# The neighbourhood values of two hybrid layers projected beside the first differential head

## The chip, the core and the metric

The kernel runs on one core of a Trainium2 chip. The core has a matrix engine (PE, with a weight loader PEld), a vector engine (DVE), a scalar engine (ACT), a general engine (POOL), and a queue of transfers that the kernel issues on SP. Each engine works through its own list of instructions in order and waits where an instruction needs what another engine has not finished. The metric is the time of one execution in microseconds; a change is judged by the median of several executions.

## The reference, cut to what matters

Two layers of a hybrid mixer (sequence 1024, width 1024) are followed by a second network that the change does not touch. A layer projects its normalized input once, splits the result, runs three attentions and projects their gated outputs back:

```python
proj = h @ w_in
c_q, c_kv, k_pe, na_qkv, diff_qkv, g_mla, g_na, g_diff = jnp.split(proj, IN_SPLITS, axis=-1)
...
qn, kn, vn = jnp.split(na_qkv, 3, axis=-1)          # 6 heads of 64
o_na = neighborhood_attention(qn, kn, vn, na_rpb, NA_DIM ** -0.5)
...
qd, kd, vd = jnp.split(diff_qkv, 3, axis=-1)        # 4 heads, 2 x 32 for q and k, 64 for v
# per block of 128 queries:
s = jnp.einsum('bqhnd,bkhnd->bhnqk', qi, k) * scale
p = jax.nn.softmax(s, axis=-1)
a = p[:, :, 0] - lam * p[:, :, 1]
o = jnp.einsum('bhqk,bkhe->bqhe', a, v)
```

`vn`, the neighbourhood values, is `h` times 384 columns of `w_in`. The differential attention needs only `qd`, `kd` and `vd`; the neighbourhood attention, which comes after it in the kernel, is the first to need `vn`.

## The kernel before

Everything is a chain of stages. A stage has items (one step of the outer loop each) and a preparation (loads and splits of weights, loads of queries and keys) that runs spread over the items of the stage ahead of it. An item is a generator: at each step of the chain the new item runs to its first `yield`, and then every unfinished older item runs on to its next `yield` (`lane`, `step`). So a `yield` inside an item means "one item later". A stage may carry a side lane: another list of stages whose items are stepped in even proportion between the items of the main lane; what is left of it is run out when the main stages it is tied to end (`run`).

The order that this writes down is not quite the order in which the engines work. The build sorts each engine's instructions by a simulated timeline (`schedule_with_timeline_sim=True`): an instruction that is written later but ready earlier may go first, and the written order is a priority. Each engine then keeps to that list on the chip.

In a hybrid layer `project1` returns eight projection stages: lat, gate1, gate0, dv, dqk, nq, nk, nv. The last, nv, has 8 items, one for each 128 rows. An item multiplies its rows by the 384 columns: eight blocks of the sum, each as three products of high and low parts, 24 matmuls of 128x384. Its result lies in one half of a PSUM tile named S (`acc` hands out the two halves of one tile to two items in turn); one item later `v_store` copies it out with two ACT casts and two DVE subtractions and stores it. All projections read the layer's input `hT`, 16 SBUF pages; the split weights of nv take 8 pages more. The pool `pg` has 43 pages in all.

After the projections come 4 differential heads, 6 neighbourhood heads and 6 latent heads. A differential head has 16 items: 8 blocks of 128 queries, two items for each, one for either softmax. An item issues two score matmuls into an S tile (there are two S tiles), then DVE takes the row minimum into a page P, one item later ACT takes the exponential and POOL rescales. With the second item of a block POOL adds the two pages (for blocks 0, 3 and 6 of a head DVE does it, one item later). Then the block, called a tile below, waits `lag` items, PE transposes it in 8 matmuls and ACT copies the transposes out; `lag2` items later, for each second block, PE multiplies the pair by the values (16 matmuls in the trace, which shows each as two). The lines of the profile that belong to this are L289 (projection), L297 and L298 (casts and subtractions of the store), L1073 (scores), L793 (row minimum), L796 (exponential), L801 and L1080 (rescaling and addition on POOL), L1083 (addition on DVE), L816 and L822 (transposes and their copies) and L842 (values).

The preparation of the stage nv holds its 4 weight loads and splits, and in layer 0 a quarter of the modulation steps, in layer 1 a quarter of the steps that build tables for the second network. The preparation of head 0 holds constants (6 small loads that keep their order), queries, keys, values and gates, and in layer 1 five further table steps (`step_m`, `step_w`, `step_e`, `step_lv`, `step_k`).

Of the kernel before, what the change touches and what calls it, by code (L numbers as in the profile page):

```python
# [56 lines left out]
def bcast(ap, n=128):  # L57

    return bass.AP(tensor=ap.tensor, offset=ap.offset, ap=[[0, n]] + list(ap.ap))
# [101 lines left out]
class Net:  # L161
# [878 lines left out]
    def diff_stages(self, i, D, mixT):  # L1040
        nc, I = self.nc, self.I
        lam_init = 0.8 - 0.6 * math.exp(-0.3 * i)
        C = {}

        def consts():
            lv = self.small([128, 4, 32], name="lamv")
            for j, nm in enumerate(("lam_q1", "lam_k1", "lam_q2", "lam_k2")):
                self.dma(lv[:, j, :], bcast(I[nm][i]), True)
            lp = self.small([128, 2, 32], name="lamp")
            ls = self.small([128, 2], name="lams")  # L1050
            nlam = C["nlam"] = self.small([128, 1], name="nlam")
            nc.vector.tensor_mul(lp[:, 0, :], lv[:, 0, :], lv[:, 1, :])
            nc.vector.tensor_mul(lp[:, 1, :], lv[:, 2, :], lv[:, 3, :])
            nc.vector.reduce_sum(ls, lp, axis=AX.X)
            nc.scalar.activation(ls, ls, AF.Exp)
            nc.vector.tensor_sub(nlam, ls[:, 1:2], ls[:, 0:1])
            nc.vector.tensor_scalar_add(nlam, nlam, -lam_init)
            sg = C["sg"] = self.small([128, 1], name="subg")
            for e in range(2):
                self.dma(sg[e * 64:e * 64 + 64], I["subln_g"][i].unsqueeze(1), True)  # L1060
            nc.vector.tensor_scalar_mul(sg, sg, 1.0 - lam_init)

        def loads(h, T):
            def one(s):
                T["q", s] = self.head_rows(D["dqk"], 2 * h + s, 32, (0, 0, 1, 1), "dqT")
                T["k", s] = self.head_rows(D["dqk"], 8 + 2 * h + s, 32, (0, 1, 0, 1), "dkT")
            return [lambda s=s: one(s) for s in range(2)]

        def tile(h, T, qt, X, s):
            qs = slice(qt * 128, qt * 128 + 128)  # L1070
            sp = self.big()
            for c in range(2):
                nc.tensor.matmul(sp[:, c, :], T["q", s][:, qs], T["k", s][:, c * 512:c * 512 + 512], start=True, stop=True)  # L1073
            X[s] = yield from self.softmax_rows(sp)
            if s == 1:
                (P0, f0), (P1, f1) = X.pop(0), X.pop(1)
                self.rescale(P1, f1, C["nlam"])
                if qt % CM:
                    self.rescale(P0, f0)
                    nc.gpsimd.tensor_add(P0, P0, P1)  # L1080
                else:
                    yield
                    nc.vector.scalar_tensor_tensor(P0, P0, f0, P1, op0=ALU.mult, op1=ALU.add)  # L1083
                X["P"] = P0

        def sub(M):
            sq = self.half(name="dsq")
            nc.scalar.activation(sq, M, AF.Square)
            yield
            p = self.mm()  # L1090
            nc.tensor.matmul(p, self.sub, sq, start=True, stop=True)
            yield
            nc.scalar.activation(sq, p, AF.Ln, bias=self.eps)
            nc.scalar.activation(sq, sq, AF.Exp, scale=-0.5)
            yield
            nc.vector.tensor_mul(M, M, sq)
            nc.vector.tensor_scalar_mul(M, M, C["sg"])
        st = self.attn_stages(4, 6, loads, tile, self.full_pair, D["dv"], D, mixT, sub=sub, subs=2, plain=True, lag=9, lag2=3)
        st[0].prep.insert(0, consts)
        return st  # L1100

# [58 lines left out]
    def block1(self):  # L1160
        I = self.I
        src = I["x"][0]
        hT = FeatT(self, "hT")
        mods = [self.scratch([3, 1024], name=f"mods{i}") for i in range(2)]
        hx, C = {}, {}

        def ldx(t, src=src):
            hx[t] = self.page(name="h")
            self.dma(hx[t], src[t * 128:t * 128 + 128])

        def ldm(i):
            C["A"], C["B"] = self.rows(mods[i][1], "mA"), self.rows(mods[i][0], "mB")

        def ldgate(i):
            C["gate"] = self.rows(mods[i][2], "mg")

        def ldln():
            C["A"], C["B"] = self.rows(I["ln_mix_even_2"][0], "mA"), None
        P, loads, products, ends = self.ada_rows()
        early = []  # L1180
        D, st = self.project1(0, hT, early)

        begun = {}

        def norm0(t, hT=hT):
            return self.norm_item(t, lambda t: hx.pop(t), lambda: C["A"], lambda: C["B"], hT)()

        def begin(t):
            begun[t] = norm0(t)
            for _ in range(3):  # L1190
                next(begun[t])
        pre = [self.ada_silu] + loads + [lambda: ldx(0)] + early[1:5] + [lambda t=t: ldx(t) for t in range(1, 4)]
        pre += [lambda: C.update(P)] + products + [early[0], self.setup_rope] + [lambda t=t: ldx(t) for t in range(4, NT)] + [lambda: begin(0)] + early[5:] + [lambda: begin(1)] + ends
        stages = [Stage(pre, [lambda t=t: begun.pop(t) if t in begun else norm0(t) for t in range(NT)], "norm")]
        for i in range(2):
            if i == 1:
                D, st = self.project1(i, hT)
            nf, E = self.na_bias(i)
            st[3].prep += nf
            stages += st  # L1200
            if i == 0:
                ad = self.ada_steps(0, mods[0], (2,)) + self.ada_steps(1, mods[1])
                for j in range(4, 8):
                    st[j].prep += ad[(j - 4) * len(ad) // 4:(j - 3) * len(ad) // 4]
            mixT = FeatT(self, "mx")
            df = self.diff_stages(i, D, mixT)
            na = self.na_stages(D, mixT, E)
            ml = self.mla_stages(D, mixT)
            if i == 1:
                T = self.s5_scratch()  # L1210
                tb, steps = self.s5_tables(T)
                steps = [steps[j * 5:j * 5 + 5] for j in range(4)]
                for j in range(4):
                    st[4 + j].prep = self.mixed(st[4 + j].prep, tb[j * len(tb) // 4:(j + 1) * len(tb) // 4])
                df[0].prep += steps[0]
            stages += df + na + ml
            hs = self.scratch([S, 1024], name=f"h{i}")
            setattr(self, f"h{i}", hs)
            nhT = FeatT(self, "hT")

            def fin(t, h, nhT=nhT, hs=hs):
                self.dma(hs[t * 128:t * 128 + 128], h)
                yield
                x = yield from self.norm_scale(h, C["A"], C["B"])
                yield
                self.turn(x, t, nhT)

            so = self.out_stages(I["w_out"][i], mixT, lambda: C["gate"], src, fin)
            if i == 1:
                so[1].prep += steps[1]  # L1230
                self.s5_later = [("v1", steps[2]), ("q0", steps[3])]
            so[0].prep.insert(0, lambda i=i: ldgate(i))
            so[1].prep.append((lambda: ldm(1)) if i == 0 else ldln)
            stages += so
            src, hT = hs, nhT
        return stages, src, hT, T
# [785 lines left out]
```

## Time and profile before

| | |
|---|---|
| median of 3 runs | 4135.8 us (4135.6 to 4144.27) |
| the profiled execution | 4136.66 us, its span 4134.9 us |
| PE, PEld busy | 3929.0 us (95%), 3349.6 us (81%) |
| DVE busy | 2600.4 us (63%) |
| ACT, POOL busy | 1834.0 us (44%), 1829.3 us (44%) |
| mean granted clock of PE | 0.973 |

The shares are means over a program of many stages. A matmul counts as busy from its start to a modelled end, and matmuls overlap, so PE's share says little about how tightly it is packed; the distance from one start to the next does. The granted clock is 1.00 at 2.4 GHz; PE runs at that or at half of it, and a value between is a mean over time.

### The profile page before, as it was taken

To read this page: it belongs to the slowest core of one execution; us is meant where nothing else is said; L and a number is where in the kernel's file an instruction comes from. 1 tells how busy PE (TensorE), PEld (TensorE's weight loads), DVE (VectorE), ACT (ScalarE), POOL (GpSimd) and SP (SyncE) were. 2 spreads that over 40 slices of the span, in tenths; PEclk is the share of its full clock that TensorE was granted. 3 is DMA by queue.
4 is the path that set the end of the run, shared out by engine and by line. 5 is a ranking of instruction groups with operands and counts; after the bars stand their busy time and mean duration, and the time that the engine had idled before them with its cause. 6 is when DMAs were issued, how large, how long until landed. Compare 5 with 4: busy or idle time off the path is not lost. (4 is left out here: it accounts for less than half of the span.)

```text
span 4134.9 us, 59445 instructions
## 1 busy us (share of the span) xinstructions
PE 3929.0 (95%) x21519; PEld 3349.6 (81%) x21519; DVE 2600.4 (63%) x5041; ACT 1834.0 (44%) x3867; POOL 1829.3 (44%) x1514
## 2 busy tenths in 40 slices
PE   8999889999998899999978999999999899999999
PEld 7889568988886579888867778888879788888879
DVE  6767768836786778645677644555575744555573
ACT  6643777726445777432465421111135621111145
POOL 3442765635434854512256444434433154434433
PEclk9999999999999999998888999999999999999999
DMA  5567333333536243335344311111111111111111
GB/s 180 148 203 240 99 113 115 93 128 118 174 108 175 72 139 92 123 117 179 95 161 133 126 48 46 51 46 51 52 47 52 42 50 48 52 45 53 57 42 56
DMA packets 379517, 410.47 MB, mean 99 GB/s; under 512 B 68265, under 2 KB 304457, under 8 KB 379224
## 3 DMA queue, kind: packets, MB, share of 16 engines
q1 hardware_dynamic: 379224, 406.67, 31.9%
q8 instruction: 171, 2.80, 0.3%
q14 instruction: 122, 1.00, 0.1%
HBM read 300.43 MB, written 106.18 MB: 98 GB/s over the span
## 5 line engine op out<-in xcount | busy, mean ns | idle before, releaser
L294 POOL TENSOR_TENSOR wl<-wr,wh 128x1024 fp32r<-128x1024 f32 (+4 forms) x262 | 606.4, 2320 | 1168.0 <-ACT wh L293 729.6
L1804 DVE TENSOR_TENSOR h<-h,mm 128x512 f32<-128x512 f32 x512 | 352.2, 688 | 658.2 <-PE mm L289 658.2
L289 PE MATMUL S<-hT,wh 128*128 128x512 f32 x2176 | 688.3, 390 | 3.8 <-ACT hT L297 1.5
L289 PE MATMUL S<-wh,hT 128*128 128x256 f32 (+3 forms) x2304 | 563.1, 329 | 9.1 <-DVE vst L298 3.1
L293 ACT CAST wh<-wr 128x1024 fp32r<-128x1024 f32 (+4 forms) x264 | 262.5, 1000 | 501.3 <-PE tp L289 246.9
L289 PEld LDWEIGHTS S<-hT,wh 128*128 128x128 f32 x2176 | 408.0, 188 | 90.9 <-ACT hT L297 2.3
L289 PEld LDWEIGHTS S<-wh,hT 128*128 128x128 f32 x2304 | 404.3, 193 | 25.1 <-issue 6.7
L289 PE MATMUL S<-hT,wl 128*128 128x512 f32 x1088 | 423.7, 389 | 0.0
L289 PE MATMUL S<-wl,hT 128*128 128x256 f32 (+3 forms) x1152 | 373.4, 324 | 0.6 <-POOL wl L294 0.6
L1804 DVE TENSOR_TENSOR h<-h,tp 128x512 f32<-128x512 f32 x512 | 352.1, 688 | 22.3 <-PE tp L289 22.3
L1788 ACT ACTIVATE z<-S 128x512 f32<-128x512 f32 x128 | 69.6, 596 | 634.4 <-PE S L289 634.3
L816 PE MATMUL tp<-c,P 128*128 128x128 f32 x2000 | 291.9, 281 | 41.0 <-DVE PTl L298 17.5
L801 POOL TENSOR_SCALAR P<-P,sx 128x1024 f32<-128x1024 f32 (+2 forms) x232 | 231.7, 1004 | 203.9 <-DVE sx L797 76.1
L298 DVE TENSOR_TENSOR PTl<-tp,PTh 128x512 fp32r<-128x512 f32 (+3 forms) x432 | 253.2, 608 | 89.3 <-ACT PTh L297 84.6
L816 PEld LDWEIGHTS tp<-c,P 128*128 128x128 f32 x2000 | 236.1, 144 | 90.3 <-issue 22.8
L793 DVE CUSTOM_DVE_ANT_1 P<-S,zero 128x1024 f32<-128x1024 f32 x224 | 266.7, 1216 | 30.3 <-PE S L1073 27.2
L796 ACT ACTIVATE P<-P,sx 128x1024 f32<-128x1024 f32 x224 | 258.6, 1158 | 39.0 <-DVE sx L793 28.1
L297 ACT CAST PTh<-tp 128x512 fp32r<-128x512 f32 (+3 forms) x432 | 215.8, 530 | 114.9 <-PE tp L816 111.9
L289 PEld LDWEIGHTS S<-hT,wl 128*128 128x128 f32 x1088 | 204.3, 188 | 42.1
L289 PEld LDWEIGHTS S<-wl,hT 128*128 128x128 f32 x1152 | 223.1, 194 | 6.1 <-POOL wl L294 0.9
L289 PE MATMUL mm<-wh,hT 128*128 128x256 f32 x1152 | 221.7, 285 | 2.2 <-DVE hT L298 1.7
L1790 POOL TENSOR_TENSOR z<-z 128x512 f32<-128x512 f32 x128 | 130.7, 1043 | 196.4 <-ACT zh L1789 196.4
(451 smaller groups left out, 9494.5 us busy)
## 6 DMA issues: line engine op xcount, KB each, us to landing
wr<-in_w_mlp_up_dram SPq DMA_DIRECT2D x64, 512.0 KB
wr<-in_w_mlp_down_dram SPq DMA_DIRECT2D x64, 512.0 KB
adw<-in_ada_w_dram SPq DMA_DIRECT2D x48, 512.0 KB
h<-h SPq DMA_DIRECT2D x32, 512.0 KB
wr<-in_w_in_dram SPq DMA_DIRECT2D x28, 512.0 KB
wr<-in_w_in_dram SPq DMA_DIRECT2D x24, 384.0 KB
mqT<-mq SPq DMA_DIRECT2D x24, 384.0 KB
mkT<-mk SPq DMA_DIRECT2D x24, 384.0 KB
```

The lines of the kernel that those rows point to most:

```text
L289: self.nc.tensor.matmul(ps, a, b, start=(i == 0), stop=(i == n - 1))
L293: self.nc.scalar.copy(hi, src)
L294: (eng or self.nc.gpsimd).tensor_sub(lo, src, hi.bitcast(F32))
L297: self.nc.scalar.copy(hi, ps)
L298: self.nc.vector.tensor_sub(lo, ps, hi.bitcast(F32))
L793: nc.vector.tensor_tensor_reduce(P.rearrange("p (a b) -> p a b", a=2), Sv, self.zero.unsqueeze(2).to_broadcast([128, 2, 512]), 1.0, 3.0e38 ...
L796: nc.scalar.activation(P, P, AF.Exp, bias=nm[:, 0:1], scale=-1.0, accum_out=nm[:, 1:2])
L801: self.nc.gpsimd.tensor_scalar(P, P, f, g, op0=ALU.mult, op1=ALU.mult)
L816: self.nc.tensor.transpose(tp[:, j, :], P[:, b * 128:b * 128 + 128], self.eye)
L1788: nc.scalar.activation(z, p[:, n, :], AF.Relu)
L1790: nc.gpsimd.tensor_mul(z, z, z)
L1804: nc.vector.tensor_add(H[t][:, sl], H[t][:, sl], o)
```

## The change

In both layers the stage nv is taken from the end of the projections. Its preparation is put in front of that of head 0, so both now run in the items of nk. Its items become a side lane of head 0. Since head 0 has 16 items and the side lane counts 10 steps, a step of the side lane stands after items 2, 4, 5, 7, 8, 10, 12, 13, 15 and 16 of head 0. The five table steps of layer 1 move from the preparation of head 0 to that of head 1, which runs in head 0's items. For all four heads of both layers `lag` goes from 9 to 5 and `lag2` from 3 to 2.

```diff
-        st = self.attn_stages(4, 6, loads, tile, self.full_pair, D["dv"], D, mixT, sub=sub, subs=2, plain=True, lag=9, lag2=3)
+        st = self.attn_stages(4, 6, loads, tile, self.full_pair, D["dv"], D, mixT, sub=sub, subs=2, plain=True, lag=5, lag2=2)
         st[0].prep.insert(0, consts)
         return st
...
                 for j in range(4):
                     st[4 + j].prep = self.mixed(st[4 + j].prep, tb[j * len(tb) // 4:(j + 1) * len(tb) // 4])
-                df[0].prep += steps[0]
+                df[1].prep += steps[0]
+            nv = stages.pop()
+            df[0].prep = nv.prep + df[0].prep
+            df[0].side = ([Stage([], nv.items)], 1)
             stages += df + na + ml
```

## Rows read from the trace of the kernel before

**Rows 1.** Windows: length; PE, PEld, DVE, ACT, POOL busy (instructions); clock; DMA share, GB/s.
```profile
382.00:416.30 34.30, 34.30 (x198) 32.39 (x197) 11.80 (x35) 9.25 (x28) 0.00 (x0) 1.00 0.85 249
416.30:442.40 26.10, 19.75 (x72) 11.06 (x71) 22.94 (x50) 20.09 (x37) 16.46 (x12) 0.80 0.79 192
442.40:474.40 32.00, 30.08 (x154) 19.25 (x153) 26.27 (x49) 27.06 (x49) 31.45 (x19) 1.00 0.30 75
474.40:516.40 42.00, 37.75 (x171) 22.64 (x170) 29.23 (x57) 31.83 (x59) 32.49 (x21) 0.96 0.19 51
516.40:555.00 38.60, 34.99 (x170) 22.35 (x170) 27.95 (x56) 31.33 (x58) 31.72 (x24) 0.96 0.32 90
...
1250.00:1288.00 38.00, 34.88 (x219) 34.25 (x218) 17.80 (x41) 6.93 (x20) 0.00 (x0) 0.96 0.68 218
1288.00:1317.40 29.40, 19.76 (x79) 11.65 (x79) 23.43 (x50) 21.54 (x39) 19.33 (x13) 0.88 0.75 181
...
1347.60:1391.00 43.40, 37.90 (x175) 23.18 (x174) 29.16 (x58) 32.30 (x58) 34.47 (x22) 0.96 0.17 49
```

**Rows 2.** Timeline of PE where it is packed: start, duration, line, shapes, count.
```profile
448.58 1.94 PE L842 MATMUL mm<-PTp,V 128*64 128x256 f32 x8
450.45 1.20 PE L1073 MATMUL S<-dkT,dqT 128*128 128x512 f32 x4
451.49 1.13 PE L816 MATMUL tp<-c,P 128*128 128x128 f32 x8
452.51 0.73 PE L1073 MATMUL S<-dkT,dqT 128*128 128x512 f32 x2
```

**Rows 3.** Groups by shape in 416.3 to 442.4 us, those of PE.
```profile
L1073 PE MATMUL S<-dkT,dqT 128*128 128x512 f32 x31 | 13.8, 538 | 5.8 <-DVE sx L793 5.7
...
L816 PE MATMUL tp<-c,P 128*128 128x128 f32 x24 | 4.1, 320 | 0.6 <-POOL P L1080 0.6
L842 PE MATMUL mm<-PTp,V 128*64 128x256 f32 x16 | 3.7, 382 | 0.0
```

**Rows 4.** Timeline of PE at its waits, in brackets the idle time before.
```profile
416.29 0.63 PE L1073 MATMUL S<-dkT,dqT 128*128 128x512 f32 x2
419.13 1.14 PE L1073 MATMUL S<-dkT,dqT 128*128 128x512 f32 x2 [2.22 <-DVE sx L793]
...
427.97 1.81 PE L816 MATMUL tp<-c,P 128*128 128x128 f32 x8
...
491.06 0.74 PE L1073 MATMUL S<-dkT,dqT 128*128 128x512 f32 x2 [0.47 <-DVE sx L793]
...
1275.91 0.57 PE L289 MATMUL S<-wh,hT 128*128 128x384 f32 x1 [3.12 <-DVE vst L298]
...
1309.54 1.07 PE L816 MATMUL tp<-c,P 128*128 128x128 f32 x8 [1.11 <-POOL P L1080]
```

**Rows 5.** Groups by shape in 1288 to 1317.4 us, those of PE.
```profile
L1073 PE MATMUL S<-dkT,dqT 128*128 128x512 f32 x32 | 12.6, 499 | 8.2 <-DVE sx L793 8.2
L816 PE MATMUL tp<-c,P 128*128 128x128 f32 x29 | 4.8, 307 | 1.5 <-POOL P L1080 1.5
```

**Rows 6.** Timeline of DVE: two additions, one table operation.
```profile
426.61 1.31 DVE L1083 SCALAR_TENSOR_TENSOR P<-P,sx 128x1024 f32<-128x1024 f32 x1
...
499.29 3.35 DVE L1083 SCALAR_TENSOR_TENSOR P<-P,sx 128x1024 f32<-128x1024 f32 x1 [4.35 <-POOL P L801]
...
1824.70 2.88 DVE L1461 TENSOR_TENSOR s5w<-s5ea,s5bc 128x512 f32<-128x512 f32 x1
1827.51 0.68 DVE L1463 TENSOR_TENSOR s5M<-s5ea,s5bc 128x512 f32<-128x512 f32 x1
```

**Rows 7.** Timeline of POOL: one addition, one subtraction.
```profile
507.30 2.69 POOL L1080 TENSOR_TENSOR P<-P 128x1024 f32<-128x1024 f32 x1
...
1824.19 2.85 POOL L294 TENSOR_TENSOR wl<-wr,wh 128x1024 fp32r<-128x1024 f32 x1
```

## The prediction

> **What bounds the kernel now.** I read the windows by stretch first, then the groups by shape, then the timelines of PE, DVE and POOL. The change lives in the two hybrid layers, so their stretches are cut there: projection of the neighbourhood values (382 to 416.3 us and 1250 to 1288 us), the first differential head (to 442.4 and 1317.4), the heads after it [rows 1]. In the projection PE is full and the others rest: in layer 0 PE is busy all 34.3 us, POOL not at all, DVE 11.80 and ACT 9.25 us. In the head behind it that turns round: of 26.1 us PE shows 19.75 busy, at a mean clock of 0.80, while DVE has 22.94. The two stand one behind the other though neither needs the other. Layer 1 repeats it.
>
> A busy PE is not a packed PE, so its work is priced by starts. In the projection 198 instructions fill 34.30 us, 0.173 each [rows 1]. Four score matmuls take 1.04 us from the first start to what follows (0.26 each), eight transposes 1.02 (0.128 each), eight value matmuls 1.87 (0.234 each) [rows 2]. The first head's stretch of layer 0 holds 31, 24 and 16 of these [rows 3]: 8.1 + 3.1 + 3.7 = 14.9 us of work in 26.1. So 11.2 us of PE are lost while the head's pipeline fills: the second score pair stands 2.22 us behind DVE, and so on through the first dozen [rows 4]. Layer 1 holds 32, 29 and again 16 [rows 3, 5]: 8.3 + 3.7 + 3.7 = 15.7 in 29.4, so 13.7 lost; and its projection loses 3.12 us to a store that waits on DVE [rows 4], behind which the mean clock of 0.96 over 38 us means some 3 us at 1.2 instead of 2.4 GHz, 1.5 us more [rows 1]. What better cover could win is 11.2 + 13.7 + 4.6 = 29.5 us. The heads after it take 32.0, 42.0 and 38.6 us in layer 0; by the same prices a whole head is 32 scores, 64 transposes, 64 value matmuls, 31.5 us, so the second runs at PE's speed and the third loses some 10 us.
>
> **The change, part by part.** *The projection beside head 0.* The 192 matmuls cost PE 192 x 0.173 = 33.3 us as before: none is removed. Head 0 has 16 items and the side lane 10 steps, so from the second item on a projection (4.2 us of PE) stands behind about every second score pair. Head 0 then needs 34.3 + 14.9 = 49.2 us of PE instead of two stretches of 60.4. Other engines: ACT 9.25 + 20.09 = 29 us, DVE 11.80 + 22.94 = 35, POOL 16.46 [rows 1], all below 49, so the stores' casts and subtractions cost nothing; PE's work hides them, and without it DVE would be next.
>
> *The S tiles.* The projection takes halves of the same two S tiles of PSUM that the scores use. A pair of projections holds one from its first matmul to its second store, and four pairs fill most of head 0, so scores then alternate through one tile. What that costs the trace shows once: 2.84 us from the first score pair to the second, when stores still held a tile, with 2.22 us of PE wait, and waits of 0.4 to 0.5 us later, when the head has both [rows 4]. Behind a projection there is no wait (4.2 us cover the 2.84). Eight of 16 scores have no projection in front: nothing each at best, up to 8 x 2.2 = 17.6 us per layer at worst. The build orders every engine's instructions by a simulated timeline, and may put ready projections into these gaps; I take 5 us per layer, nearer to none, since PE has 33 us of independent work.
>
> *The preparation.* What prepared the projection (4 weight loads with their splits, a quarter of the modulation or table steps) already ran in the key projection's items; what prepared head 0 ran in the value projection's and now shares the same 8 items. That moves 16 DMAs (8 of queries and keys, values, gate, 6 small constants), some 2.9 MB, past the key projection's stores on SP, and six tiny operations; POOL gets none. At the 249 GB/s of the stretch they leave [rows 1], 2.9 MB are 11.6 us. If they land late, scores start late, but PE has projections: nothing, at most 11.6 us if the planner puts scores first. I take 0. The 5 table steps of layer 1 move from the projection into head 0's items: 18 DVE operations of about 0.68 us, 40 PE instructions, 3 us. They filled DVE when the store came 3.12 us late; spread out I count them at nothing more. The values are first needed by the neighbourhood heads, which begin behind the differential ones at 555 us, long after.
>
> *Pages.* The 16 pages of the input and 8 of the split weights live through most of head 0 instead of ending at its start, out of 43. Fewer score pages are then free. The shorter wait gives back two tiles' worth. Cost 0, up to the whole gain if pages run out; no row prices it.
>
> *The wait, 9 to 5 and 3 to 2.* This holds for all four heads of both layers. A tile's transposes are written 10 items after its second score now, 6 after the change (one more where DVE adds). At 139 us for 64 items (416 to 555) that is 13.0 us instead of 21.7. A tile is ready between 8.8 us after its second scores (419.13 to 426.61 + 1.31) and 18.9 (491.06 to 507.30 + 2.69) [rows 4, 6, 7]; the 30 tiles of layer 0 that I followed lie between, half above 12.8. So half the tiles would not be ready at their written place. But the written place is only a priority: the very first transposes went out after the 7th score pair, where the text has 13. What remains is the planner's error: where transposes already run as soon as ready, PE waited up to 1.11 us for POOL [rows 4], and not at all for tile 0. From zero to 1.1 us per tile; heads 1 to 3 have 24 tiles and 112.6 - 94.5 = 18 us of PE slack per layer, 0.75 per tile. I take it as hidden. Two tiles and about two pairs fewer (some 6 us of PE) remain to fill the start of the neighbourhood heads: 1 us per layer lost.
>
> The sum: -29.5 + 2 x 5 + 2 x 1 = -17.5, on the profiled 4136.7 us, is 4119; that execution is 0.9 above the median of 4135.8, so 4118.
>
> A rule that speaks against the moved table steps. By the row, a table operation that takes 0.68 us alone took 2.88 us when it began 0.5 us into a POOL subtraction of 2.85 us [rows 6, 7]. The Trainium skill (SBUF — State Buffer, the section on who contends with whom) says that a VectorE instruction with two SBUF inputs and a GpSimd one that reads SBUF exclude each other for a whole instruction; that row agrees. Without it the sum stays 4119, with it it is 4128, the fourth rival.
>
> **The rivals.** *Slower: POOL is late for five items.* PE, in order, stands before each tile in heads 1 to 3. For it: ready at 8.8 to 18.9 us against 13.0. Against: the plan moves with readiness, and 0.75 us per tile of slack. At 0.7 us on all 48 tiles, unhidden, 33.6 us: 4119 + 33.6 = 4152. It eats the gain from 0.36 us per tile and makes it slower by 0.2% from 0.54.
>
> *No change: the S tiles.* Eight exposed scores per layer at 1.3 us of wait, the middle of 0.47 and 2.22, are 10.4 us per layer: -29.5 + 20.8 + 2 gives 4130, and worse if pages run short too, 4130 to 4140. For it: only two tiles. Against: projections are ready filling.
>
> *Better: the third head's hole goes too.* At 493 to 504 us DVE stood 4.35 us before an addition that waited for POOL and then took 3.35 [rows 6], PE ran dry and the clock fell (0.96 over the stretch). The stretch takes 42.0 against 31.5 of work; layer 1 has the same hole (43.4) [rows 1]. A shorter wait lets PE take transposes there instead of new scores. If 8 us in each layer vanish: 4103.
>
> *Table steps collide with POOL.* 18 operations, POOL busy about 55% of the time, 2.2 us lost each: 22 us more on DVE in layer 1's head 0, to 17.80 + 23.43 + 22 = 63 against 67.4 - 13.3 = 54: 9 us given back, 4128.
>
> **How the numbers follow.** Forecast 0.50, better 0.13, table steps 0.05, S tiles 0.17, POOL late 0.15. A measurement of this kernel tells about 0.2% (8.3 us) from no change: faster is below 4127.5, slower above 4144. Faster: 0.13, 0.47 of the forecast's 0.50, half of the table steps and a little of the S tiles, 0.65; same 0.20; slower 0.15. Likeliest alone: 4108 to 4126. The range for 8 in 10 reaches below the better case (4098) and to a half-hidden POOL wait (4146).
>
> **What would show it.** Right: scores begin near 383 and near 1250 us, among projection matmuls; PE's clock stays at 1.00 there; 16 score pairs and all eight projections end in about 50 to 54 us instead of 60.4 (layer 0) and 67.4 (layer 1); heads 1 to 3 of layer 0 keep about 113 us. Wrong: PE idle before L816 released by POOL in most tiles; idle before L1073 of over 10 us among the projections; DVE's L793 waiting for POOL (pages); table operations of 2 us and more on DVE. The prediction fails if the heads after the first lengthen by more than the fill gives.

## The result: slower by 0.7%, and the profile after

The changed kernel takes 4164.97 us in the median of 6 runs (4159.3 to 4173.48), the kernel before 4135.7 in 6 runs beside it (4131.78 to 4144.27): a ratio of 1.0069, interval 1.0054 to 1.0084. Forecast were 4118 us and a range of 4098 to 4146. The profiled execution of the changed kernel took 4173.48 us, 8.5 above its median, and its span is 36.7 us longer than that of before.

Where those 36.7 us arise is read from the timelines of PE, as the starts of the first score pair of head 0, of the 17th pair (head 1 begins), of the first neighbourhood score and of the first latent score (us):

| kernel, layer | head 0 | head 1 | neighbourhood | latent |
|---|---|---|---|---|
| before, layer 0 | 416.3 | 443.3 | 555.0 | 668.7 |
| changed, layer 0 | 388.8 | 467.7 | 583.5 | 686.5 |
| before, layer 1 | 1288.0 | 1318.4 | 1428.2 | 1536.6 |
| changed, layer 1 | 1262.7 | 1346.6 | 1464.3 | 1565.6 |

Scores begin 27.5 and 25.3 us earlier, as the change means them to, and head 1 begins 24 and 28 us later. At the first latent score layer 0 has lost 17.8 us, at that of layer 1 the loss is 29.0, as large as that of the medians. The other 7.7 us of this execution come in parts that the change does not touch. There is one trace of each kernel, and behind the first latent score of layer 1 the traces of this study differ by up to 12 us, so marks that differ by a few us show little.

The windows of the changed kernel answer to [rows 1], cut at its own starts of a head. The first and the fifth row shown are head 0 with its lane:

```profile
388.80:467.70 78.90, 60.67 (x315) 52.43 (x313) 37.68 (x93) 32.57 (x74) 22.42 (x15) 0.91 0.47 127
467.70:502.50 34.80, 33.19 (x153) 20.13 (x154) 23.00 (x51) 26.05 (x48) 25.49 (x18) 0.95 0.57 140
502.50:543.60 41.10, 34.76 (x166) 20.94 (x165) 34.04 (x58) 32.67 (x60) 31.37 (x18) 1.00 0.22 59
543.60:583.50 39.90, 34.00 (x161) 21.39 (x159) 26.34 (x51) 27.38 (x49) 31.39 (x23) 0.91 0.30 85
...
1262.70:1346.60 83.90, 66.99 (x356) 58.55 (x354) 47.24 (x108) 34.46 (x76) 27.68 (x18) 0.88 0.44 132
```

Head 0 with its lane takes 78.9 and 83.9 us where the prediction wanted 50 to 54. PE is busy for 60.67 and 66.99 of them; the clock that should have stayed at 1.00 is 0.91 and 0.88. The three heads behind it take 115.8 us in layer 0 and 117.7 in layer 1, against 111.7 and 109.8 by the same marks before.

The groups by shape in 388.8 to 467.7 us (last columns: busy, mean ns, idle before and its releasers) answer to [rows 3]:

```profile
L289 PE MATMUL S<-wh,hT 128*128 128x384 f32 x128 | 36.1, 357 | 2.6 <-DVE sx L793 2.6
L289 PE MATMUL S<-wl,hT 128*128 128x384 f32 x64 | 22.6, 354 | 0.0
L1073 PE MATMUL S<-dkT,dqT 128*128 128x512 f32 x32 | 11.7, 447 | 12.2 <-DMA dkT<-dqk 7.7 <-DVE sx L793 4.5
L842 PE MATMUL mm<-PTp,V 128*64 128x256 f32 x32 | 7.3, 382 | 0.0
L816 PE MATMUL tp<-c,P 128*128 128x128 f32 x48 | 7.1, 277 | 1.0 <-ACT PTp L822 1.0
```

Priced by starts as in the prediction this is 192 x 0.173 + 32 x 0.26 + 32 x 0.234 + 48 x 0.128 = 33.2 + 8.3 + 7.5 + 6.1 = 55.1 us, and 1.4 for 11 transposes of the key projection. So 78.9 us hold 56.5 of work, 16.9 of idle time (these rows and 1.1 before a transpose), and 5.5 that neither explains; the slow clock below fits them. All 192 matmuls of the projection and all 16 score pairs are in it, but 6 tiles too, where before has 3.5 at the end of head 0: part of the late head 1 is work done earlier.

The list of waits of PE names the idle time (us in total, times, longest); first layer 0, 380 to 470 us, then layer 1, 1255 to 1348:

```profile
PE S L1073 <- DMA dkT<-dqk: 7.7, 1, 7.7
PE S L1073 <- DVE sx L793: 5.8, 5, 1.4
PE mm L481 <- DVE acc L476: 3.3, 1, 3.3
PE S L289 <- DVE sx L793: 2.6, 2, 1.3
```
```profile
PE S L1073 <- DMA dkT<-dqk: 5.2, 1, 5.2
PE S L1073 <- DVE sx L793: 4.9, 3, 1.9
PE S L289 <- DVE sx L793: 2.7, 2, 1.3
PE S L1502 <- DVE sx L793: 1.5, 1, 1.5
```

Two causes carry most of it: keys that land late, 7.7 + 5.2 = 12.9 us, and S tiles that wait for DVE's row minimum, 8.4 in layer 0 and 9.1 in layer 1. The kernel before has 5.7 and 8.2 us of this second wait in its head 0 [rows 3, 5]: the lane was to fill them, and did not. The places of both in the timeline of PE, layer 0 (it answers to [rows 4]):

```profile
384.67 2.41 PE L481 MATMUL mm<-acc,ones 128*1 128x512 f32 x4 [3.29 <-DVE acc L476]
...
399.10 1.19 PE L1073 MATMUL S<-dkT,dqT 128*128 128x512 f32 x2 [7.71 <-DMA dkT<-dqk]
400.09 0.52 PE L289 MATMUL S<-wh,hT 128*128 128x384 f32 x1
400.41 0.52 PE L289 MATMUL S<-wl,hT 128*128 128x384 f32 x1
...
414.91 0.44 PE L289 MATMUL S<-wh,hT 128*128 128x384 f32 x1 [1.32 <-DVE sx L793]
...
426.65 0.73 PE L1073 MATMUL S<-dkT,dqT 128*128 128x512 f32 x2 [1.32 <-DVE sx L793]
428.71 0.44 PE L289 MATMUL S<-wh,hT 128*128 128x384 f32 x1 [1.32 <-DVE sx L793]
```

PE's list has the second score pair ahead of the projections. PE works in order: it stands 7.71 us for keys with the whole lane behind it, since no projection of the lane has begun. When it goes on, projections start 0.32 us apart instead of 0.173 until 403 us, half speed. From 412 on a pattern repeats where two score pairs stand between projections: the second pair waits for the row minimum of the pair before, and then the next projection waits for the row minimum of that second pair, because it needs a tile that the scores hold.

The queue on SP shows why the keys are late (start, duration, transfer, count):

```profile
379.91 0.62 SPq L279 DMA_DIRECT2D dkT<-dqk  x1
...
388.88 0.42 SPq L279 DMA_DIRECT2D lamv<-in_lam_q_dram  x1
...
391.07 0.53 SPq L279 DMA_DIRECT2D nk<-xT  x1
391.65 0.55 SPq L279 DMA_DIRECT2D dqT<-dqk  x1
392.30 1.39 SPq L279 DMA_DIRECT2D dkT<-dqk  x2
```

Head 0 has four key transfers, two for each softmax. The two of the first softmax are issued by 379.91 us. The two that the second score pair needs are issued together at 392.30, behind modulations, constants and a store of the key projection. The queue's own list of waits, 378 to 400 us, says what held it longest:

```profile
SPq L279 <- ACT ado L485: 6.0, 2, 5.5
```

This is the store of the modulation. The queue works in order too: the store waits for ACT's copy of what L481 makes, and L481 had waited 3.29 us for DVE. So in layer 0 the late modulation step delays the keys as well, and the two waits are one chain. Layer 1 has no modulation step there; constants and stores of the key projection stand ahead of its keys, and the wait is shorter.

### The profile page after: what moved, and what is told of

Same layout as the page of the kernel before. It is cut to its first block, busy times and chain, and to the rows that moved or that the text cites. A ratio compares the mean times of both kernels' runs of the same rounds, so it can differ in the third digit from the quotient of the medians.

```text
span 4171.6 us, 59456 instructions
## 1 busy us (share of the span) xinstructions
PE 3936.9 (94%) x21519; PEld 3360.2 (81%) x21519; DVE 2607.3 (63%) x5041; ACT 1832.8 (44%) x3867; POOL 1827.2 (44%) x1514
## 5 line engine op out<-in xcount | busy, mean ns | idle before, releaser
L289 PE MATMUL S<-wh,hT 128*128 128x256 f32 (+3 forms) x2304 | 570.9, 332 | 10.9 <-DVE sx L793 5.3
L816 PE MATMUL tp<-c,P 128*128 128x128 f32 x2000 | 285.2, 278 | 38.7 <-DVE PTl L298 10.0
L816 PEld LDWEIGHTS tp<-c,P 128*128 128x128 f32 x2000 | 232.9, 142 | 80.2 <-issue 17.1
```

Source lines behind the costliest of these rows:

```text
L289: self.nc.tensor.matmul(ps, a, b, start=(i == 0), stop=(i == n - 1))
L816: self.nc.tensor.transpose(tp[:, j, :], P[:, b * 128:b * 128 + 128], self.eye)
```

## The experiments

Theory A: the lane makes the loss. Theory B: the shorter wait makes it. Ratios are to the runs of the kernel before on the same chip, whose medians were 4133.83 (first four), 4137.41 (next four), 4137.29 and 4138.02 us. Line numbers differ by a few between these kernels, since an edit adds lines above; the names of the tiles are the same.

**The lane alone.** The changed kernel with the old waits.

```diff
-        ... plain=True, lag=5, lag2=2)
+        ... plain=True, lag=9, lag2=3)
```


> The lane alone, waits as before (9 and 3). Theory A (the lane costs: PE stands for loads at its start and for a free S tile in it, while the shorter wait gives some 10 us per layer back in the neighbourhood heads): slower than the changed kernel, 4175 to 4190 us, with the stretch from the projection to the 16th score pair at 80 us and more in layer 0. Theory B (the forecast's slower rival: the wait of 5 is too short, the lane itself gains): faster than before, 4105 to 4120 us, that stretch at 50 to 54 us.

Measured: 4175.33 us (4173.15 to 4181.09), 1.0097 (1.0079 to 1.0115). The lane makes the whole loss and 10 us more.

**The wait alone.** The kernel before with waits of 5 and 2.

```diff
-        ... plain=True, lag=9, lag2=3)
+        ... plain=True, lag=5, lag2=2)
```


> The shorter waits alone, the projection as a stage of its own as before. Theory A: faster than before by 10 to 25 us (4111 to 4126), the neighbourhood heads some 10 us shorter per layer, heads 1 to 3 about 112 us. Theory B: slower, 4145 to 4170 us, with PE idle before transposes that POOL releases.

Measured: 4144.17 us (4138.77 to 4150.16), 1.0018 (1.0007 to 1.0029). B falls as the main cause, and with it A's own part that the wait alone would gain. In layer 0 heads 1 to 3 take 119.7 us instead of 111.7: head 1 is 3.4 us shorter, heads 2 and 3 are 6.3 and 5.1 us longer. The windows of these two:

```profile
478.10:524.70 46.60, 40.08 (x187) 24.77 (x188) 34.08 (x63) 34.76 (x64) 34.95 (x22) 0.96 0.20 56
524.70:567.20 42.50, 37.15 (x163) 22.49 (x162) 25.64 (x51) 28.16 (x50) 32.73 (x24) 0.88 0.28 76
```

The neighbourhood heads then take 103.1 us instead of 113.7; that fewer tiles are left for them is the likely reason. The hole of the third head of before is not closed, as the "better" rival had it: PE's longest wait for a row minimum there comes earlier (at 486.3 instead of 493.5 us) and grows from 1.7 to 2.3 us. At the first latent scores the trace has lost 1.7 us in layer 0 and 2.8 in layer 1.

**Sums in tiles of their own.** The changed kernel; the projection sums in a tile of the other PSUM tag and leaves both S tiles to the scores.

```diff
+            own = self.mm() if nh == 6 else None
-            p = self.proj(hT, W, t, nh * 64).rearrange(...)
+            p = self.proj(hT, W, t, nh * 64, own).rearrange(...)
```


> The changed kernel, but the projection's sums lie in PSUM tiles of the other pool, so that scores keep both S tiles. Theory A1 (the shared S tiles are the larger part of the lane's cost, 1.3 us at some eight score pairs per layer): 4140 to 4150 us, and no waits of 1.3 us before score pairs in head 0. Theory A2 (the late loads at the start are the larger part): 4158 to 4168 us, waits of 1.3 us replaced by others.

Measured: 4146.34 us (4136.39 to 4153.68), 1.0029 (1.0018 to 1.004): 18.6 us of the loss gone. Its waits of PE in layer 0, 380 to 450 us:

```profile
PE S L1074 <- ACT P L797: 3.9, 1, 3.9
PE mm L481 <- DVE acc L476: 3.3, 1, 3.3
...
PE S L1074 <- DVE sx L794: 1.3, 2, 0.8
```

The S waits fall from 8.4 to 1.3 us (in layer 1 from 9.1 to 3.8), and no projection of the lane waits for a row minimum. The waits for keys are shorter too. The 3.9 us stand before the same second score pair; the list names ACT, whose exponential ended last, but the later of this pair's two key transfers, issued at 391.01, lands at 396.2, within 0.1 us of that end. PE's list has one whole projection (24 matmuls, 388.0 to 392.4 us) ahead of this pair now, and it covers the rest of the wait. In layer 1 the keys cost 1.2 us instead of 5.2. So 7.8 us of waits for keys went beside the 12.4 of the S tiles, and not all 18.6 us belong to the tiles. This profile is of the kernel's fastest run.

**Keys earlier.** The changed kernel; head 0's preparation runs one stage earlier, in the items of nq.

```diff
-            df[0].prep = nv.prep + df[0].prep
+            stages[-1].prep += df[0].prep
+            df[0].prep = nv.prep
```


> The changed kernel, but the preparation of head 0 runs one stage earlier (in the items of the neighbourhood queries). Theory A2 (late loads): PE does not stand for the keys of head 0, 12 us less in layer 0 and 5 in layer 1, 4143 to 4152 us. Theory A1: 4160 to 4168 us, the loads' wait gone but the time lost again at the S tiles.

Measured: 4151.32 us (4148.04 to 4162.76), 1.0042 (1.0027 to 1.0058): 13.7 us gone. The waits in layer 0, 380 to 472 us:

```profile
PE mm L481 <- DVE acc L476: 6.6, 1, 6.6
PE S L1073 <- DVE sx L793: 5.2, 5, 1.9
PE S L289 <- DVE sx L793: 4.2, 3, 1.6
```

No wait for a transfer is left. The S waits stay, at 9.4 us, and PE now stands 6.6 us before the modulation step instead of 3.3; its last weights are issued at 386.26 us on SP, where the changed kernel issues them at 373.29. So that 13.7 is near the 12.9 that the keys cost is partly chance: layer 0 reaches its latent heads at 686.2 us, as in the changed kernel (686.5), and all that the trace gains up to the latent heads of layer 1, 7.7 us, lies in layer 1. This profile is of the kernel's slowest run.

**Both, with either wait.** The two edits above together, first with waits of 5 and 2, then of 9 and 3.

> The changed kernel with two edits that were tried singly before: the projection sums in tiles of its own (-18.6 us alone) and head 0's queries, keys and constants loaded one stage earlier (-13.7 us alone), with the waits of 5 and 2. Theory A (the lane loses by the shared S tiles and by the late keys, two separate places): the gains add up, 4165 - 18.6 - 13.7 = 4133, no slower than the kernel before. Rival C (both are one loss seen twice: the start of the lane gets slow in any case, and what one edit gives back the other can't): about the better of the two, 4143 to 4150. Rival D (the forecast's fill is real and was only hidden): 4120 or less.

> As the run with both edits, but with the old waits of 9 and 3. If the short wait costs beside a lane what it cost without one (4144.2 against 4133.8, with an interval of 0.07 to 0.29%), this is 7 us faster than that run: theory A 4126, rival C 4136 to 4143. If the short wait helps beside the lane, as the lane alone with the old wait suggested (4175.3 against 4165), it is 10 us slower: 4143 (A).

Measured: 4133.29 us (4131.22 to 4141.56), 0.9991 (0.9981 to 1.0001), and 4134.72 (4126.06 to 4139.06), 0.9988 (0.9979 to 0.9998). By the medians the two gains add up, 31.7 us against 18.6 + 13.7 = 32.3, so rival C falls. The traces do not divide the 31.7 us between two separate places, since tiles of their own shorten the waits for keys as well. The whole loss is gone, and the fill is not there. The old wait makes no difference here.

**And the modulation moved**, from the items ahead of the lane into head 0's, with either wait.

```diff
-                for j in range(4, 8):
+                for j in range(4, 7):
                     st[j].prep += ad[(j - 4) * len(ad) // 4:(j - 3) * len(ad) // 4]
+                late = ad[3 * len(ad) // 4:]
...
+            else:
+                df[1].prep += late
```


> As the run with both edits (waits 5 and 2), and in layer 0 the last quarter of the modulation steps is moved from the items before the lane into head 0's items, since with the keys early PE stood 6.57 us before a modulation step that waited for DVE. Theory A: 3 to 6 us less than that run, about 4128. If the modulation steps only move their wait into the lane or head 0: the same as that run.

> As the run before with the modulation moved, but with the old waits of 9 and 3. This would be the forecast's own lane, with its own tiles, keys in time and no modulation step ahead of it. Theory A: about 4120 to 4123, faster than the kernel before by over 0.2%. If the lane can at best come out even, because head 0 fills PE only while the projections last and its tiles then spill into the heads after it: 4130 to 4136.

Measured: 4136.89 us (4132.92 to 4142.76), 0.9998 (0.9989 to 1.0006), and 4126.03 (4119.38 to 4137.0), 0.9976 (0.9964 to 0.9988). The second is the best kernel of this study, 11.4 us faster than before. Its windows of head 0 with the lane:

```profile
385.60:433.80 48.20, 45.94 (x255) 41.95 (x252) 41.39 (x84) 26.60 (x60) 25.43 (x14) 1.00 0.74 225
1244.30:1301.70 57.40, 52.92 (x304) 48.88 (x302) 46.48 (x98) 29.37 (x64) 25.96 (x16) 0.94 0.51 158
```

This is the lane as forecast: 48.2 us, at a clock of 1.00. And yet layer 0 gains nothing. Head 1 begins at 433.8 instead of 443.3, but only 2 tiles are transposed by then and no values multiplied, against 3.5 tiles and 16 value matmuls before: 1.5 x 1.02 + 3.7 = 5.2 us of the 9.5 are work handed on. The neighbourhood heads begin at 557.0 (before 555.0), the latent heads at 669.0 (668.7). Layer 1 reaches its latent heads at 1527.1 (1536.6).

**Without the lane.** Three kernels made from before, with its waits: the modulation of layer 0 and the table steps of layer 1 moved into head 0's items; the projection's sums in tiles of their own; both.

```diff
-                df[0].prep += steps[0]
+                df[1].prep += steps[0]
+            else:
+                df[1].prep += late
```
(`late` is cut out as in the edit before, and the tiles are those of the run with tiles of their own.)

> The kernel before with no lane and the old waits, but the five table steps of layer 1 and the last quarter of the modulation steps of layer 0 moved into head 0's items, as in the best kernel so far (4126.0). If that kernel's gain over before (10 us, nearly all of it in layer 1) comes from the moved steps and not from the lane: 4126. If it is the lane's: 4136. In between: the shares of the two.

> The kernel before with no lane and the old waits; only the projection of the neighbourhood values sums in tiles of its own instead of halves of S. In the trace of before the stores of the last projections cost the first score pair 2.2 us per layer, so at most 2 x 2 us are there to win: 4133 to 4137. If it gains far more, the 18.6 us that the same edit gave beside the changed kernel's lane were not due to the lane.

> The two edits of the runs above together (moved steps and own tiles), no lane, old waits: all of the best kernel so far except the lane itself and the loads that it needs earlier. Its distance to that kernel (4126.0) is the lane alone. If the lane fills PE as forecast: 4136 here, 10 us slower. If the lane is worth nothing even when repaired: 4126.

Measured: 4180.29 us (4179.89 to 4181.66), 1.0106 (1.009 to 1.0121); 4137.41 (4129.94 to 4144.29), 1.0000 (0.9991 to 1.0009); 4186.41 (4184.0 to 4196.24), 1.0124 (1.011 to 1.0138). The first lies 44 us above the highest value expected: neither theory had a price for moved steps. The first kernel's windows of head 0, layer 0 and 1, and its waits of PE in layer 1, 1306 to 1359 us:

```profile
413.30:452.10 38.80, 20.36 (x49) 10.48 (x47) 32.59 (x58) 20.11 (x36) 23.64 (x13) 0.60 0.47 162
1306.30:1358.00 51.70, 30.26 (x112) 19.08 (x110) 40.55 (x75) 24.56 (x45) 28.05 (x18) 0.60 0.23 76
```
```profile
PE S L1073 <- DVE sx L793: 13.8, 7, 4.7
PE tp L1491 <- DVE s5M L1468: 3.9, 1, 3.9
PE tp L1510 <- DVE s5R L1508: 2.8, 1, 2.8
```

Without projections to run, PE waits for a DVE that is busy 32.59 of 38.80 us, and its clock is 0.60. Head 0 takes 38.8 and 51.7 us instead of 27.0 and 30.4. At the first latent scores layer 0 has lost 26.0 us and layer 1 another 18.8, which is all of the loss. Against the third kernel, which has the same steps and tiles, the lane (with its earlier keys) is worth 60 us; against before, which has the steps elsewhere, 11.4. The tiles by themselves are worth nothing without a lane, so the 18.6 us above are what they give beside one.

**The lane over two heads.** The kernel with everything moved and waits of 5 and 2, its lane spread over heads 0 and 1.

```diff
-            df[0].side = ([Stage([], nv.items)], 1)
+            df[0].side = ([Stage([], nv.items)], 2)
```


> The repaired lane with waits of 5 and 2 (own tiles, early keys, late modulation, 4136.9), but spread over the items of the first two heads: a projection step behind every fourth score pair or so. If PE's idle time in head 0 is what the lane can fill and it is full already, this is 4137 again or a little slower, since pages live longer. If the projections were too dense (PE full in head 0, so the head's tiles spill into heads 1 to 3, where PE then loses time of its own), the same work over two heads fills more: 4125 to 4130.

Measured: 4170.59 us (4166.99 to 4171.83), 1.008 (1.0066 to 1.0094): 34 us slower than over one head (4136.89). Its windows of heads 0 and 1, layer 1:

```profile
1253.50:1332.60 79.10, 50.26 (x229) 39.49 (x226) 43.19 (x89) 27.48 (x57) 24.37 (x16) 0.74 0.31 95
1332.60:1385.90 53.30, 52.88 (x284) 40.38 (x284) 27.78 (x63) 33.27 (x66) 26.48 (x18) 1.00 0.36 100
```

In head 0, with the table steps and half of the projection's matmuls (96 of 192), PE idles for 29 us; in head 1 it is full. Nearly all of the loss lies in layer 1: against the lane over one head layer 0 reaches its latent heads 6.5 us later, and layer 1 loses another 28.1. So the dense lane is needed where the table steps run; layer 0, with modulation steps in their place, shows little of it.

**The table steps left in place.** First the changed kernel, then the best one, with the five table steps of layer 1 in the items ahead of head 0. With a lane these are the items of nk, no longer those of nv, so the steps share them with the preparation of the projection. (In the best kernel the steps are put behind `nv.prep` where that is set.)

```diff
-                df[1].prep += steps[0]
+                df[0].prep += steps[0]
```


> The changed kernel, with only the five table steps of layer 1 left where they were (in the items before head 0, not in head 0's). Without a lane, steps moved into head 0 made layer 1 about 19 us longer from its first item to its last latent score, and the modulation steps moved there made layer 0 26 us longer. Theory S (the moved table steps fill DVE in the changed head 0 too and are part of its loss): 4165 - 10 to 19 = 4146 to 4155, all of it in layer 1. Theory A (beside the lane head 0 is bound by the S tiles, and DVE has room): 4165, or a little more because the steps then stand before the first scores.

> The best kernel so far (lane with its own tiles, early keys, late modulation, waits of 9 and 3: 4126.0), with the table steps of layer 1 left in the items before head 0. If DVE has room beside the repaired lane, the steps are covered in head 0 and putting them back costs the time by which they delay the projections, 3 to 5 us (before lost 3.12 us to a store that waited for DVE there): 4129 to 4131. If they cost in head 0 also beside the lane: 4116 to 4122.

Measured: 4168.79 us (4167.4 to 4170.83), 1.0074 (1.0061 to 1.0087), and 4147.67 (4142.48 to 4153.26), 1.0025 (1.0017 to 1.0034). In the changed kernel the moved steps are no part of the loss (1.0069 with them): theory S falls. They make head 0 of layer 1 longer, 83.9 us against 73.8 without them, but with the steps ahead the first scores come 12 us later, at 1274.6. In the best kernel putting them back costs 21 us, more than expected, and makes it slower than the kernel before: the repaired lane gains only together with the moved steps. The timeline of PE there, just ahead of head 0:

```profile
1246.92 1.76 PE L1495 MATMUL tp<-c,s5M 128*128 128x128 f32 x8 [3.75 <-DVE hss L336]
...
1253.78 4.11 PE L1506 MATMUL S<-s5bc,s5W 64*128 64x16 f32 x32 [4.46 <-DVE s5W L1469]
```

PE stands 8.2 us before matmuls of two table steps, which its list has ahead of the first scores; these begin 14.0 us later than in the best kernel. By the latent heads of layer 1 the trace has lost 12.6 us; the other 10 come behind them and stay unexplained.

## Why the prediction was wrong, point by point

**The step that failed first: "If they land late, scores start late, but PE has projections: nothing, at most 11.6 us if the planner puts scores first. I take 0."** The planner put scores first. Keys landed late in both layers, 7.7 and 5.2 us of PE, and loading them earlier gave back 13.7 by the medians. The 11.6 us were worked out and then not taken: independent work covers a late transfer only if it stands ahead of the waiting instruction in its engine's list. The kernel with tiles of its own shows it from the other side: with one projection ahead of the same score pair the wait in layer 0 was 3.9 us. No term had the modulation step either, 3.3 us before L481. In layer 0 it held the queue and so the keys; with the keys early PE stood 6.6 us before it, and the trace gained nothing in that layer.

**The S tiles were mis-sized.** Taken: 5 us per layer, nearer to none. Measured: 8.4 and 9.1 us of waits; with both tiles left to the scores 12.4 us of these waits went, with 7.8 of the waits for keys, and 18.6 of the time. Wrong was "behind a projection there is no wait": the projection itself waits, since it needs a tile that a score holds, and so where two pairs stand between projections PE waits twice, 0.5 to 1.9 us before the second pair and 1.3 before the projection (two places in each layer). The mechanism was the "no change" rival's, nearly at its price of 10.4 per layer. The Trainium skill (Perfetto Trace Analysis, the section Optimization Strategy) says that one gap that repeats on the engine that should be full can mean that there is no SBUF or PSUM for the next tile. The trace agrees: 1.32, 1.32 and 1.32 us in the timeline above, and the tiles of their own removed them.

**"PE's clock stays at 1.00 there" failed with them.** It was 0.91 and 0.88. With two levels, a mean of 0.91 over 78.9 us is 14 us at 1.2 GHz, which cost at most 7.1 us where PE was busy, and 0.88 over 83.9 at most 10.1; both bounds are high, because part of the slow time was idle. In the best kernel, with neither keys nor tiles late, it was 1.00 and 0.94.

**The table steps at nothing: right for the change as a net sum, and not for the reason given.** Spreading them out was not enough: without a lane beside them the same move, with that of the modulation steps, cost 43 us. In the changed kernel head 0 of layer 1 paid some 10 us for them, and the scores came 12 us earlier. The rival by which they collide with POOL was not what cost the changed kernel: 4168.79 us with the steps left in place.

**The wait: hidden, 1 us per layer lost.** By itself it cost 10.3 us between the medians (0.18%, 0.07 to 0.29%) instead of 2 for both layers; the trace shows 4.5 of them in the two layers. The rival "POOL is late" had the sign and not the mechanism: in heads 1 to 3 of the changed kernel's layer 0 POOL's addition holds L816 for 3.4 us in 2 waits, not 0.7 us on each of 24 tiles, and the neighbourhood heads are 10.7 us shorter (103.0 instead of 113.7). Beside the lane its sign changes: 10 us gained in the changed kernel, nothing with two edits, 10.9 lost with three. Why it helps in one and not in another stays open.

**The fill of 29.5 us.** With keys, tiles and modulation out of the way and the old wait back, the forecast's deductions for tiles and wait fall away, and all 29.5 us should have been there. Measured were 11.4 (0.12 to 0.36%), nearly all in layer 1, and none without the moved table steps. In layer 0 the premise failed: the idle PE time of head 0, 11.2 us, can be filled, and nearly was (45.94 of 48.20 us busy), but more than half of the earlier end was tile work handed to heads that lose PE time of their own (123.2 us from head 1 to the neighbourhood in the best kernel, 111.7 before). An idle stretch of one stage is not a gain until what follows can use it.

**The pages at nothing** held: in the differential heads of the changed kernel no row minimum of DVE waits for POOL to give a page back.

By the medians 47.0 us lie between forecast and result. Keys 12.9, S tiles 17.5 - 10 = 7.5 more than taken, the modulation step and a key transpose 4.4, and the clock at most 17.2 make at most 42.0. Against them stand the 10 us that the shorter wait gave beside this lane; so by this estimate 15 us or more are fill that was counted and not there. Idle time and slow clock overlap, and so do keys, modulation and tiles, so the shares within this stay open; that the two edits together give back 31.7 us is measured.

## What to carry to other kernels

When independent work is put beside a stage to fill it, ask three things first: what stands ahead of the filling in the engine's own list and what it waits for (the queue of transfers is such a list too), which buffers the filling shares with the stage that it fills, and whether the stage's own work is done sooner or only handed on. A bound that was worked out for a late transfer belongs in the sum unless the list itself shows that other work stands ahead of it. And a step that is free beside a dense lane can cost some 19 us beside none, so the edits of one change are to be priced together.

## What the runs showed of the hardware

By their times DVE and POOL held each other up, both ways, in the kernel with moved steps and no lane. Its timeline of DVE in layer 0, then that of POOL:

```profile
434.82 2.12 DVE L467 SCALAR_TENSOR_TENSOR acc<-adw,ada_s,acc 128x1024 f32<-128x1024 f32 x1
436.86 1.21 DVE L793 CUSTOM_DVE_ANT_1 P<-S,zero 128x1024 f32<-128x1024 f32 x1
...
443.89 1.26 DVE L1083 SCALAR_TENSOR_TENSOR P<-P,sx 128x1024 f32<-128x1024 f32 x1
445.08 1.28 DVE L467 SCALAR_TENSOR_TENSOR acc<-adw,ada_s,acc 128x1024 f32<-128x1024 f32 x1
```
```profile
433.49 2.37 POOL L1080 TENSOR_TENSOR P<-P 128x1024 f32<-128x1024 f32 x1
...
442.94 1.12 POOL L801 TENSOR_SCALAR P<-P,sx 128x1024 f32<-128x1024 f32 x1 [0.32 <-DVE sx L797]
444.07 3.19 POOL L801 TENSOR_SCALAR P<-P,sx,nlam 128x1024 f32<-128x1024 f32 x1
```

The modulation step at 434.82 starts inside an addition of POOL that ends at 435.86 and takes 2.12 us, to 1.1 after that end. The one at 445.08, directly behind an addition on DVE, takes 1.28, the middle of this kernel's 28 such steps; there POOL's rescaling, begun 0.18 us after DVE's addition, lasts 3.19 us, to 0.9 after the step, where the middle of the 64 of its form is 1.20. The prediction had priced only DVE's side of this. The row minimum, which reads PSUM, took 1.20 to 1.21 us throughout.
